# One decoder layer on one core: MLP up projection in pairs of output tiles by Strassen's scheme

## The chip, the cores and the metric

The kernel runs on one core of a Trainium2 chip. The metric is device time in microseconds (us). The times of the kernel before, from three runs, are 928.68, 927.98 and 928.27 us, median 928.27. The engines are named PE (matrix products), DVE (vector), ACT (scalar functions), POOL (GpSimd) and SP (issues DMAs). PSUM is the memory that PE adds into, in banks of 512 fp32 columns; SBUF holds everything else on chip.

## The reference, cut to what matters

```python
xn = rms_norm(h, g_mix[i])
z = xn @ w_in[i]
...
h = h + (gate_a * ya + gate_b * yb) @ w_o[i]
hn = rms_norm(h, g_mlp[i])
h = h + jnp.square(jax.nn.relu(hn @ w_up[i])) @ w_down[i]
gp = jax.nn.sigmoid(rms_norm(h, g_ple[i]) @ w_ple_gate[i])
h = h + gp * (p[i] @ w_ple_proj[i])
```

There is one layer, 1024 channels, an MLP of 4096, and 576 tokens (512 of a prompt and 8 x 8 samples). `w_up` is 1024 x 4096 and `w_down` 4096 x 1024. Everything is fp32.

## The kernel before

Channels lie on partitions and tokens on columns, in two halves of 288. `product` (L104) makes one output tile of 128 channels x 576 tokens: for each of 8 k tiles it does three matmuls, since every fp32 operand is split into two parts, hi + lo, and hi x hi, hi x lo and lo x hi are added up (`mm`, L99). Each matmul is done for both halves, into two banks of one PSUM tile. So a tile takes 8 x 3 x 2 = 48 matmuls of 128 x 288. Four PSUM tiles of two banks take turns.

The weights of one output tile are one unit, 128 x 1024, read from memory by SP (`load_unit`, L81). `split` makes hi on ACT (L70) and lo on DVE (L71). Four raw units and three split ones fit. `Stream.next` splits two units ahead of use and loads one more ahead. So the order in which units stand in `order` and the place of `next()` in the program set when ACT and DVE split, between the other work on their queues. Each engine runs its queue in the order of the program.

Stages, with their stretch in the profiled execution: the first products, k by k as the loads land (0 to 31 us), the convolution branch (31 to 160), its gate and projection (160 to 262), the pooling branch (262 to 390), w_o (390 to 434), then the MLP in four blocks of 8 up and 8 down tiles (434 to 846; the first up stage is 434 to 488, the second 539 to 590, the third 641 to 692), and the embedding gate and last norm. In the first stage, `stat.tokens()` (L235 to L244) and `stat.spread()` (L251) make 1/rms of each token between the products: sums on PE, then a chain of small operations on ACT and DVE, then PE spreads them.

In w_o the residual is added by DVE (L404) and the operand of the MLP is made by `split_act` with the gain (L73, L74). In an up tile ACT takes the relu from PSUM (L421), DVE squares it (L423), and it is split (L70, L71). A down tile is added up on DVE (L437).

## Time and profile before

| | before |
|---|---|
| median of 3 runs | 928.27 us |
| profiled execution, span | 926.5 us |
| PE busy | 913.4 us, 99% of the span |
| DVE busy | 431.6 us, 47% |
| ACT busy | 289.8 us, 31% |
| POOL busy | 98.3 us, 11% |
| bytes by SP's queue | 79.98 MB, 26.4% of the DMA engines' time |

The time of the profiled execution itself is given only as its span, from the first to the last instruction. PE's clock is at its full level in all of the 40 slices but the last. Busy times count what an engine works on; an engine with a low share can still hold up another, if the order on its queue is unlucky. The chain of waits is followed from the last instruction back, so a long piece of it on one engine means that this engine had no gap there.

### The profile page before, as it was taken

The numbers are of one execution on the slowest core, as the hardware profiler recorded it, in microseconds if no ns is written. First come the engines' busy times: TensorE is split into PE (matmuls) and PEld (weight loads), VectorE is DVE, ScalarE is ACT, GpSimd is POOL, SyncE is SP. The second block draws the span as 40 slices with busy tenths as digits, with TensorE's granted clock in tenths as the row PEclk, the third lists the DMA queues.
The fourth block names the chain that finished last, engine by engine and source line by source line (L and its number), as shares of the span: only waits on it lengthen the run. The fifth ranks groups of instructions, "written<-read, shape, count | busy, mean of one in ns | idle before, by whom it ended". The sixth has DMA issues, their size and how long they took to land.

```text
span 926.5 us, 15543 instructions
## 1 busy us (share of the span) xinstructions
PE 913.4 (99%) x6842; PEld 911.5 (98%) x6842; DVE 431.6 (47%) x570; ACT 289.8 (31%) x384; POOL 98.3 (11%) x118
## 2 busy tenths in 40 slices
PE   8999999999999999999999999999999999999995
PEld 7999999999999999999999999999999999999995
DVE  7645445333246687743342133332443334567555
ACT  6422212322113222333433233211331133335532
POOL 5110001000011221023000000000000000021253
PEclk9999999999999999999999999999999999999997
DMA  6422222322322222322222222222222222222102
GB/s 227 155 92 76 84 92 69 94 88 73 92 61 88 68 92 96 112 79 91 69 90 71 91 79 82 91 70 91 87 73 92 74 86 92 94 92 84 54 22 82
DMA packets 26290, 80.98 MB, mean 87 GB/s; under 512 B 3312, under 2 KB 7024, under 8 KB 26224
## 3 DMA queue, kind: packets, MB, share of 16 engines
q1 hardware_dynamic: 26080, 79.98, 26.4%
q8 instruction: 53, 0.87, 0.4%
q14 instruction: 13, 0.11, 0.0%
q10 hardware_dynamic: 144, 0.03, 0.0%
HBM read 77.01 MB, written 2.99 MB: 86 GB/s over the span
## 4 chain that ended last, share of the span: by engine, by line
PE 97%; DVE 1%; issue 1%; DMA 1%; SPq 0%; DVEq 0%; ACT 0%; ACTq 0%
PE ps L99 89%; PE psg L99 6%; PE psf L99 1%; PE psn L251 1%; DVE lo L71 1%; DMA xall<-x 1%; PE psn L235 1%; DVE xall L464 0%; SPq L169 0%; DVE lo L74 0%; SPq L163 0%; DVEq L564 0%; DVE gp L491 0%; DVE xall L493 0%; DVE sq L218 0%
## 5 line engine op out<-in xcount | busy, mean ns | idle before, releaser
L99 PE MATMUL ps<-lo,hi 128*128 128x288 f32 x2064 | 442.2, 296 | 0.0
L99 PE MATMUL ps<-hi 128*128 128x288 f32 x2064 | 442.1, 296 | 0.0
L99 PE MATMUL ps<-hi,lo 128*128 128x288 f32 x2064 | 441.8, 296 | 0.0
L99 PEld LDWEIGHTS ps<-hi,lo 128*128 128x128 f32 x2064 | 332.7, 189 | 0.0
L99 PEld LDWEIGHTS ps<-lo,hi 128*128 128x128 f32 x2064 | 332.7, 189 | 0.0
L99 PEld LDWEIGHTS ps<-hi 128*128 128x128 f32 x2064 | 332.6, 189 | 0.0
L70 ACT CAST hi<-raw 128x1024 fp32r<-128x1024 f32 (+1 forms) x144 | 144.8, 1008 | 468.3 <-PE ps L99 400.9
L71 DVE TENSOR_TENSOR lo<-raw,hi 128x1024 fp32r<-128x1024 f32 (+1 forms) x144 | 169.3, 1179 | 157.0 <-ACT hi L70 150.4
L437 DVE TENSOR_TENSOR acc<-ps,acc 128x576 f32<-128x576 f32 x24 | 18.2, 758 | 74.3 <-PE ps L99 74.3
L225 POOL TENSOR_TENSOR ss<-sq 128x576 f32<-128x576 f32 (+2 forms) x5 | 7.2, 1434 | 416.4 <-ACT sq L220 416.4
L225 POOL TENSOR_TENSOR ss<-ss,sq 128x576 f32<-128x576 f32 (+2 forms) x29 | 38.5, 1327 | 70.3 <-ACT sq L220 56.8
L99 PE MATMUL psg<-hi 128*128 128x320 f32 (+1 forms) x128 | 38.1, 298 | 0.0
L99 PE MATMUL psg<-lo,hi 128*128 128x320 f32 (+1 forms) x128 | 37.9, 296 | 0.0
L99 PE MATMUL psg<-hi,lo 128*128 128x320 f32 (+1 forms) x128 | 37.9, 296 | 0.0
L71 DVE TENSOR_TENSOR lo<-a,hi 128x576 fp32r<-128x576 f32 x32 | 24.3, 759 | 23.6 <-ACT hi L70 23.6
L70 ACT CAST hi<-a 128x576 fp32r<-128x576 f32 x32 | 21.6, 675 | 43.6 <-DVE a L423 43.6
L220 ACT ACTIVATE sq<-xall 128x576 f32<-128x576 f32 (+2 forms) x39 | 22.7, 585 | 19.5 <-DVE xall L493 19.5
L74 DVE SCALAR_TENSOR_TENSOR lo<-xall,vec,hi 128x576 fp32r<-128x576 f32 x23 | 21.7, 946 | 7.9 <-ACT hi L73 7.9
L99 PEld LDWEIGHTS psg<-hi 128*128 128x128 f32 x128 | 24.3, 190 | 0.0
L99 PEld LDWEIGHTS psg<-lo,hi 128*128 128x128 f32 x128 | 24.3, 190 | 0.0
L99 PEld LDWEIGHTS psg<-hi,lo 128*128 128x128 f32 x128 | 24.3, 190 | 0.0
L423 DVE TENSOR_TENSOR a<-a 128x576 f32<-128x576 f32 x32 | 24.1, 752 | 0.0
(98 smaller groups left out, 444.3 us busy)
## 6 DMA issues: line engine op xcount, KB each, us to landing
raw<-w_in SPq DMA_DIRECT2D x45, 512.0 KB, 3.4
raw<-w_up SPq DMA_DIRECT2D x32, 512.0 KB, 3.4
raw<-w_down SPq DMA_DIRECT2D x32, 512.0 KB, 3.5
raw<-w_oc SPq DMA_DIRECT2D x8, 512.0 KB, 3.4
raw<-w_o SPq DMA_DIRECT2D x8, 512.0 KB, 3.5
raw<-w_pg SPq DMA_DIRECT2D x8, 512.0 KB, 3.5
xall<-x SPq DMA_DIRECT2D x7, 288.0 KB, 5.2
fraw<-w_first SPq DMA_DIRECT2D x8, 192.0 KB, 5.1
```

Source lines behind the costliest of these rows:

```text
L70: nc.scalar.copy(hi, src)
L71: nc.vector.tensor_tensor(out=lo, in0=src, in1=as32(hi), op=ALU.subtract)
L74: nc.vector.scalar_tensor_tensor(out=lo, in0=src, scalar=scale, in1=as32(hi), op0=ALU.mult, op1=ALU.subtract)
L99: nc.tensor.matmul(o, wt, cols(at), start=start and i == 0, stop=stop and i == 2)
L220: nc.scalar.activation(sq, t, AF.Square)
L225: nc.gpsimd.tensor_tensor(out=s, in0=self.parts[0], in1=sq, op=ALU.add)
L235: nc.tensor.matmul(sums[:, i:i + 1], a[:, h, c:c + m], ones32[:, 0:1], start=k == 0, stop=k == len(self.parts) - 1)
L251: nc.tensor.matmul(self.ps[:, h, c:c + m], self.y[:, i:i + 1].broadcast_to([m, P]), idt[:m, :m], start=True, stop=True)
L423: nc.vector.tensor_tensor(out=a2, in0=a, in1=a, op=ALU.mult)
L437: nc.vector.tensor_tensor(out=accs[j], in0=halves(ps), in1=accs[j], op=ALU.add)
```

## The change

The 8 up tiles of a block form four pairs, q and q + 4. Of a pair, the weights are two units of 128 x 1024, cut in halves of the k tiles: a and b of the first, c and d of the second. The operand is cut in halves of k and halves of the tokens. Strassen's scheme (in Winograd's form) makes the 2 x 2 block product with seven products of quarters. A quarter is 4 k tiles x 3 passes = 12 matmuls of 128 x 288 into one bank (L481), a pair so 84. The order of the products is b11, t2, t3, t1, b21 (added to the first product in its bank), the first product b11 of the next pair, t4 and b22 (added to their banks). The banks of a pair are those of two PSUM tiles, ab and cd; t2 and b11 are in ab, t3, t1, t4 and b22 in cd.

The operand's sums (t1 to t4) are made once, in w_o, by `Operand.add` (ACT: the gain; DVE: L505, L507, L508; splits L80, L502), for which w_o's outputs come in the order 0, 4, 1, 5, ... The weights' sums are made for each pair: s1 = c + d and s0 = c + a by a load on SP and a second DMA on POOL's queue that adds (L140), s2 = s1 + a on DVE (L160) and s3 = -s2 - b on DVE (L162). Seven forms are split a pair. Between the products ACT copies the first product (L519), and DVE takes the sums of products from PSUM: L532 (reads t2's bank), L534 (t3's), L536 (t1's), and after the last product L557. Then follow the relus and the square on ACT (L586 to L591).

All weights come in parts of 512 columns, eight raw and seven split ones, loaded five parts ahead. In the first pair of block 0 and in the first two down tiles of each block the last k tile's products are put later. The sums of squares are added on POOL in place, and the working buffers are pools that are closed between parts of the kernel. Two places of the diff are left out here: the same renaming of `stream.next()` to `stream.take(2)` in every other stage, and the pools' names.

```diff
+KH = D // 2
+NQ = NJ // 2
+NF = 7
...
-    wraw = ctx.enter_context(tc.tile_pool(name="wraw", bufs=4))
-    wsp = ctx.enter_context(tc.tile_pool(name="wsp", bufs=3))
-    tmp = ctx.enter_context(tc.tile_pool(name="tmp", bufs=8))
+    wraw = ctx.enter_context(tc.tile_pool(name="wraw", bufs=8))
+    wsp = ctx.enter_context(tc.tile_pool(name="wsp", bufs=NF))
...
+    def raw_tile(ap):
+        raw = wraw.tile([P, KH], F32, tag="raw", name="raw")
+        nc.sync.dma_start(raw, ap)
+        return raw
...
+        def summed(self, x, y):
+            raw = raw_tile(x)
+            nc.gpsimd.dma_start(raw, y, accum_op=ALU.add)
+            return raw
...
+    class Form:
+        def __init__(self, pair, name):
+            self.pair, self.name = pair, name
+
+        def load(self):
+            p, name = self.pair, self.name
+            if name in ("a", "b", "d"):
+                setattr(p, "r" + name, raw_tile(getattr(p, name)))
+            elif name == "s2":
+                p.rs1 = p.summed(p.c, p.d)
+            elif name == "s0":
+                p.rs0 = p.summed(p.c, p.a)
+
+        def split(self):
+            p, name = self.pair, self.name
+            if name == "s2":
+                p.rs2 = tmp.tile([P, KH], F32, tag="s", name="s2", bufs=2)
+                nc.vector.tensor_tensor(out=p.rs2, in0=p.rs1, in1=p.ra, op=ALU.add)
+            elif name == "s3":
+                nc.vector.scalar_tensor_tensor(
+                    out=p.rs2, in0=p.rs2, scalar=-1.0, in1=p.rb, op0=ALU.mult, op1=ALU.subtract)
+            return split(p.rs2 if name == "s3" else getattr(p, "r" + name), [P, KH], wsp, "w")
...
+        def take(self, n=1, live=0):
+
+            first = self.used - live
+            for i in range(n):
+                splits = min(self.used + n + NF - 1, first + NF)
+                self.fill(splits + self.loads, splits)
+            out = self.parts[self.used:self.used + n]
+            for i in range(self.used, self.used + n):
+                self.parts[i] = self.items[i] = None
+            self.used += n
+            return out
...
+    halved = [i + h * NQ for i in range(NQ) for h in range(2)]
+    for j in halved:
+        order += unit(w_o[j])
     for b in range(NFB):
-        order += [w_up[b * NJ + j] for j in range(NJ)]
-        order += [w_down[b * NJ + j] for j in range(NJ)]
-    order += [w_pp[i] for i in range(2)]
-    order += [w_pg[j] for j in range(NJ)]
-    stream = Stream(order, resident=range(len(order) - NJ, len(order) - 3))
-
-    # ---- loads: the input and the first weights by k tiles, so that products start early ----
+        pairs = [Pair(w_up[b * NJ + q], w_up[b * NJ + NQ + q]) for q in range(NQ)]
+        order += [Form(pairs[0], "a")]
+        for q in range(NQ):
+            order += [Form(pairs[q], n) for n in ("s2", "s0", "s1", "b")]
+            if q + 1 < NQ:
+                order += [Form(pairs[q + 1], "a")]
+            order += [Form(pairs[q], n) for n in ("d", "s3")]
...
+        raw = wraw.tile([P, KH], F32, tag="raw", name="fraw")
+        fraw.append(raw[:, :3 * P])
...
-    stream.fill(3, 0)
+    stream.fill(6, 0)
...
-                s = tmp.tile(self.shape, F32, tag="t", name="ss")
-                nc.gpsimd.tensor_tensor(out=s, in0=self.parts[0], in1=sq, op=ALU.add)
-                self.parts[0] = s
+                nc.gpsimd.tensor_tensor(out=self.parts[0], in0=self.parts[0], in1=sq, op=ALU.add)
...
+    def quarter(o, w, bs, ks, start, stop):
+        for k in ks:
+            wh, wl = (t[:, k * P:(k + 1) * P] for t in w)
+            hi, lo = bs[k]
+            for i, (wt, at) in enumerate(((wh, hi), (wh, lo), (wl, hi))):
+                nc.tensor.matmul(o, wt, at, start=start and k == 0 and i == 0,
+                                 stop=stop and k == NQ - 1 and i == 2, skip_group_check=True)
+    class Operand:
+        def __init__(self):
+            self.f = {n: [None] * NQ for n in ("b11", "b22", "b21", "t1", "t3", "t2", "t4")}
+            self.shared = None
+        def two(self, k, src, names):
+            parts = split(src, [P, NH, HT], acts2 if k == 0 else acts, "act")
+            for i, n in enumerate(names):
+                self.f[n][k] = tuple(t[:, i] for t in parts)
+        def add(self, k, g):
+            if k % 2 == 0:
+                self.shared = tuple(acts.tile([P, NH, HT], F32R, tag="act", name=n) for n in ("hi", "lo"))
+            self.two(k, g[:, 1:3], ("b11", "b22"))
+            hi, lo = (t[:, k % 2] for t in self.shared)
+            nc.scalar.copy(hi, g[:, 3])
+            nc.vector.tensor_tensor(out=lo, in0=g[:, 3], in1=as32(hi), op=ALU.subtract)
+            self.f["b21"][k] = hi, lo
+            t = tmp.tile([P, 4, HT], F32, tag="g", name="gt", bufs=2)
+            nc.vector.tensor_tensor(
+                out=t[:, 0:2], in0=g[:, 0:1].broadcast_to([P, 2, HT]), in1=g[:, 1:3], op=ALU.subtract)
+            nc.vector.tensor_tensor(out=t[:, 2], in0=g[:, 2], in1=t[:, 0], op=ALU.subtract)
+            nc.vector.tensor_tensor(out=t[:, 3], in0=g[:, 3], in1=t[:, 2], op=ALU.subtract)
+            self.two(k, t[:, 0:2], ("t1", "t3"))
+            self.two(k, t[:, 2:4], ("t2", "t4"))
+    def pairs_of(n, op, corner, finish, late=False, between=None):
+        def begin(w):
+            ab = psum.tile([P, NH, 512], F32, tag="ps", name="ab")
+            quarter(ab[:, 0, :HT], w, op.f["b11"], range(NQ), True, True)
+            g = tmp.tile([P, 4, HT], F32, tag="g", name="g", bufs=2)
+            nc.scalar.copy(g[:, 1], ab[:, 0, :HT])
+            return ab, g
+        ab, g = begin(stream.take()[0])
+        for i in range(n):
+            cd = psum.tile([P, NH, 512], F32, tag="ps", name="cd")
+            pa, pb, pc, pd = ab[:, 0, :HT], ab[:, 1, :HT], cd[:, 0, :HT], cd[:, 1, :HT]
+            u2 = tmp.tile([P, 1, HT], F32, tag="u", name="u", bufs=1)
+            u = u2[:, 0]
+            todo = ((pb, "t2"), (pd, "t3"), (pc, "t1"))
+            def middle(x):
+                if x == 0:
+                    nc.vector.tensor_tensor(out=u, in0=pb, in1=g[:, 1], op=ALU.subtract)
+                elif x == 1:
+                    nc.vector.tensor_tensor(out=g[:, 2], in0=pd, in1=u, op=ALU.add)
+                else:
+                    nc.vector.tensor_tensor(out=g[:, 2], in0=pc, in1=g[:, 2], op=ALU.add)
+            if late and i == 0:
+                ws = []
+                for x, (o, name) in enumerate(todo):
+                    ws += stream.take(live=x)
+                    quarter(o, ws[x], op.f[name], range(NQ - 1), True, True)
+                quarter(pa, stream.take(live=3)[0], op.f["b21"], range(NQ), False, True)
+                for x, (o, name) in enumerate(todo):
+                    quarter(o, ws[x], op.f[name], range(NQ - 1, NQ), False, True)
+                    middle(x)
+            else:
+                for x, (o, name) in enumerate(todo):
+                    quarter(o, stream.take()[0], op.f[name], range(NQ), True, True)
+                    middle(x)
+                quarter(pa, stream.take()[0], op.f["b21"], range(NQ), False, True)
+            corner(i, g, pa)
+            if i + 1 < n:
+                after = begin(stream.take()[0])
+            quarter(pd, stream.take()[0], op.f["t4"], range(NQ), False, True)
+            quarter(pc, stream.take()[0], op.f["b22"], range(NQ), False, True)
+            nc.vector.tensor_tensor(
+                out=g[:, 0::3], in0=halves(cd), in1=u2.broadcast_to([P, 2, HT]), op=ALU.add)
+            finish(i, g)
+            if i + 1 < n:
+                ab, g = after
+            if between:
+                between(i)
...
+    for x, j in enumerate(halved):
+        ps = product(stream.take(2), merged)
         nc.vector.tensor_tensor(out=xs[j], in0=halves(ps), in1=xs[j], op=ALU.add)
+        if x % 2 == 0:
+            g = tmp.tile([P, 4, HT], F32, tag="g", name="gx", bufs=2)
+        nc.scalar.mul(g[:, 2 * (x % 2):2 * (x % 2) + 2], xs[j], v(G_MLP, j))
+        if x % 2:
+            hg.add(x // 2, g)
...
+        def corner(q, g, c11):
+            nc.scalar.activation(g[:, 1], c11, AF.Relu)
+        def finish(q, g):
+            nc.scalar.activation(g[:, 0], g[:, 0], AF.Relu, scale=-1.0)
+            nc.scalar.activation(g[:, 2:4], g[:, 2:4], AF.Relu)
+            nc.scalar.activation(g, g, AF.Square)
+            sq[q] = split_act(g[:, 0:2])
+            sq[q + NQ] = split_act(g[:, 2:4])
+        def between(q):
+            if b == 0 and q == 0:
                 stat.tokens()
+            if b == 0 and q == 1:
+                stat.r2s = stat.copies(stat.spread(), "r", "rs")[1]
+        pairs_of(NQ, hg, corner, finish, b == 0, between)
...
+            if j == 0:
+                two = [stream.take(2), stream.take(2, live=2)]
+                two = [(w, psum.tile([P, NH, 512], F32, tag="ps", name="ps")) for w in two]
+                for ks in (halved[:-2], halved[-2:]):
+                    for w, ps in two:
+                        steps(ps, w, sq, ks, first=halved[0], last=halved[-1])
+            if j < 2:
+                ps = two[j][1]
+            else:
+                ps = product(stream.take(2), sq)
```

DVE near the start, before: the splits of the first weights (fraw), of the first streamed units (raw), and the chain that makes 1/rms (ms, ry, rz).

```order
L71 TENSOR_TENSOR lo<-fraw,hi 128x384 x2
L71 TENSOR_TENSOR lo<-raw,hi 128x1024
L240 TENSOR_SCALAR ms<-psn 96x6
L241 RECIPROCAL ry<-rt 96x6
L242 TENSOR_TENSOR rz<-ry 96x6
L243 SCALAR_TENSOR_TENSOR rz<-rz,ms 96x6
L244 SCALAR_TENSOR_TENSOR ry<-rz,ry 96x6
L71 TENSOR_TENSOR lo<-raw,hi 128x1024
L286 TENSOR_TENSOR c<-psf,rs 128x576
```

And now the same place:

```order
L80 TENSOR_TENSOR lo<-fraw,hi 128x384
L80 TENSOR_TENSOR lo<-raw,hi 128x512 x5
L312 TENSOR_SCALAR ms<-psn 96x6
L313 RECIPROCAL ry<-rt 96x6
L314 TENSOR_TENSOR rz<-ry 96x6
L315 SCALAR_TENSOR_TENSOR rz<-rz,ms 96x6
L316 SCALAR_TENSOR_TENSOR ry<-rz,ry 96x6
L80 TENSOR_TENSOR lo<-raw,hi 128x512
L358 TENSOR_TENSOR c<-psf,rs 128x576
```

One split of 1024 columns stood ahead of the chain, and now five of 512 do.

DVE in an up stage, before: two output tiles of the second block, weight split, square (a) and its split.

```order
L71 TENSOR_TENSOR lo<-raw,hi 128x1024
L423 TENSOR_TENSOR a_6823<-a 128x576
L71 TENSOR_TENSOR lo<-a_6823,hi 128x576
L71 TENSOR_TENSOR lo<-raw,hi 128x1024
L423 TENSOR_TENSOR a_6886<-a 128x576
L71 TENSOR_TENSOR lo<-a_6886,hi 128x576
```

Now one pair of the second block. s is the weights' sum, u and g hold sums of products, ab and cd are PSUM.

```order
L80 TENSOR_TENSOR lo<-s_6068,hi 128x512
L532 TENSOR_TENSOR u<-ab,g 128x288
L160 TENSOR_TENSOR s_6362<-raw 128x512
L80 TENSOR_TENSOR lo<-s_6216,hi 128x512
L534 TENSOR_TENSOR g<-cd,u 128x288
L162 SCALAR_TENSOR_TENSOR s_6216<-s_6216,raw 128x512
L80 TENSOR_TENSOR lo<-raw,hi 128x512
L80 TENSOR_TENSOR lo<-g,hi 128x576
L536 TENSOR_TENSOR g<-cd,g 128x288
L80 TENSOR_TENSOR lo<-g,hi 128x576
L80 TENSOR_TENSOR lo<-raw,hi 128x512 x4
L557 TENSOR_TENSOR g<-cd,u 128x2x288
```

The reads of PSUM stand between weight splits and sums of the pair after next: L160, which reads a sum made by the DMA on POOL, now stands ahead of L534.

PE in an up stage, before, with what each waits for, at the end of one tile and the begin of the next.

```order
L99 MATMUL ps_6282<-hi_5936,hi_6166 128x288 x2
L99 MATMUL ps_6282<-lo_5937,hi_6166 128x288 x2
L99 MATMUL ps_6282<-hi_5936,lo_6167 128x288 x2
L99 MATMUL ps_6338<-hi_5495,hi_6222 128x288 [waits Activation_49]
L99 MATMUL ps_6338<-hi_5495,hi_6222 128x288
L99 MATMUL ps_6338<-lo_5496,hi_6222 128x288 x2
L99 MATMUL ps_6338<-hi_5495,lo_6223 128x288 [waits DVE_49]
L99 MATMUL ps_6338<-hi_5495,lo_6223 128x288
```

Now in the second pair of the second block, at the end of t3 (into cd), where t1 (into cd) follows.

```order
L481 MATMUL cd_6192<-hi_4885,hi_6087 128x288
L481 MATMUL cd_6192<-lo_4886,hi_6087 128x288
L481 MATMUL cd_6192<-hi_4885,lo_6088 128x288
L481 MATMUL ab_6131<-hi_4416,hi_6127 128x288 [waits DVE_49]
L481 MATMUL ab_6131<-lo_4417,hi_6127 128x288
L481 MATMUL ab_6131<-hi_4416,lo_6128 128x288
L481 MATMUL ab_6131<-hi_4416,hi_6127 128x288
L481 MATMUL ab_6131<-lo_4417,hi_6127 128x288
L481 MATMUL cd_6192<-hi_4428,hi_6107 128x288 [waits DVE_49]
L481 MATMUL cd_6192<-lo_4429,hi_6107 128x288
```

A new tile waited for its weights' hi and lo; now t1 waits for a DVE operation that reads t3's bank, and five matmuls of b21 are put ahead of it, the first with a wait for DVE as well.

## Rows read from the trace of the kernel before

**Rows 1.** The page: busy time of each engine, share of the span and instructions; and the chain that ended last, its share by engine.

```profile
PE 913.4 (99%) x6842; PEld 911.5 (98%) x6842; DVE 431.6 (47%) x570; ACT 289.8 (31%) x384; POOL 98.3 (11%) x118
...
PE 97%; DVE 1%; issue 1%; DMA 1%; SPq 0%; DVEq 0%; ACT 0%; ACTq 0%
```

**Rows 2.** The chain that ended last, in order of time: start, duration (both us), engine, tile, line and count. ps is an output tile, psn the statistics, psf the first products, psg the last gate.

```profile
24.86 2.88 PE psf L99 x21
27.75 1.31 PE psn L251 x12
31.08 409.60 PE ps L99 x3072
...
449.41 403.22 PE ps L99 x3024
861.37 33.22 PE psg L99 x234
...
899.27 14.81 PE psg L99 x123
```

**Rows 3.** Windows of the second and the third up stage: the stretch, its length, then busy us and instructions of PE, PE's weight load, DVE, ACT and POOL; the granted clock of PE, the DMA share and GB/s.

```profile
539.00:590.00 51.00, 51.00 (x385) 51.00 (x384) 19.80 (x22) 17.30 (x23) 0.00 (x0) 1.00 0.26 84
...
641.00:692.00 51.00, 51.00 (x385) 51.00 (x384) 20.56 (x23) 16.97 (x22) 0.00 (x0) 1.00 0.26 83
```

**Rows 4.** Groups of instructions by line and shape: line, engine, operation, tiles and shapes, count; then busy us, mean ns of one; then idle time ahead. The splits of weights, and an operation of DVE on 512 columns with both inputs in SBUF.

```profile
L71 DVE TENSOR_TENSOR lo<-raw,hi 128x1024 fp32r<-128x1024 f32 x130 | 159.2, 1225 | 154.9 <-ACT hi L70 148.3
L70 ACT CAST hi<-raw 128x1024 fp32r<-128x1024 f32 x130 | 136.5, 1050 | 461.1 <-PE ps L99 393.7 <-issue 62.2 <-DVE lo L71 3.1
L71 DVE TENSOR_TENSOR lo<-raw,hi 128x512 fp32r<-128x512 f32 x14 | 10.1, 750 | 2.1 <-ACT hi L70 2.1
L70 ACT CAST hi<-raw 128x512 fp32r<-128x512 f32 x14 | 8.4, 619 | 7.2 <-PE ps L99 7.2
L361 DVE SCALAR_TENSOR_TENSOR pl<-q,e 128x512 f32<-128x512 f32 x8 | 5.5, 693 | 0.3
```

**Rows 5.** The same view for operations on 256 to 576 columns; the last two rows are from the timeline of DVE (start, duration), an operation and the next one.

```profile
L484 DVE TENSOR_TENSOR z<-psg,r 128x320 f32<-128x320 f32 x8 | 3.9, 491 | 8.6 <-PE psg L99 8.6
L484 DVE TENSOR_TENSOR z<-psg,r 128x256 f32<-128x256 f32 x8 | 3.4, 419 | 3.2 <-PE psg L99 3.2
L404 DVE TENSOR_TENSOR xall<-ps,xall 128x576 f32<-128x576 f32 x8 | 6.1, 758 | 26.4 <-PE ps L99 26.4
L71 DVE TENSOR_TENSOR lo<-a,hi 128x576 fp32r<-128x576 f32 x32 | 24.3, 759 | 23.6 <-ACT hi L70 23.6
L421 ACT ACTIVATE a<-ps 128x576 f32<-128x576 f32 x32 | 20.6, 644 | 0.0
L70 ACT CAST hi<-a 128x576 fp32r<-128x576 f32 x32 | 21.6, 675 | 43.6 <-DVE a L423 43.6
L220 ACT ACTIVATE sq<-xall 128x320 f32<-128x320 f32 x8 | 3.8, 471 | 9.9 <-DVE xall L493 9.9
L73 ACT ACTIVATE hi<-xall,vec 128x576 fp32r<-128x576 f32 x23 | 17.8, 773 | 19.4 <-DVE xall L440 19.3
...
902.80 1.01 DVE L464 TENSOR_TENSOR xall<-xall,r 128x640 f32<-128x640 f32 x1
903.73 0.41 DVE L493 TENSOR_TENSOR xall<-gp,xall 128x256 f32<-128x256 f32 x1
```

**Rows 6.** DMA issues: tile and source, queue, count, KB each and median us from issue to landing.

```profile
raw<-w_up SPq DMA_DIRECT2D x32, 512.0 KB, 3.4
...
xall<-x SPq DMA_DIRECT2D x7, 288.0 KB, 5.2
...
raw<-w_pool SPq DMA_DIRECT2D x4, 256.0 KB, 2.7
pin<-pt SPq DMA_DIRECT2D x2, 288.0 KB, 4.2
```

**Rows 7.** The timeline at the end of the start: start and duration in us, engine, line, operation; in brackets the idle time ahead and what ended it.

```profile
23.61 0.55 DVE L71 TENSOR_TENSOR lo<-fraw,hi 128x384 fp32r<-128x384 f32 x1
...
24.78 1.23 DVE L71 TENSOR_TENSOR lo<-raw,hi 128x1024 fp32r<-128x1024 f32 x1 [0.62 <-ACT hi L70]
...
26.35 0.16 DVE L240 TENSOR_SCALAR ms<-psn 96x6 f32<-96x6 f32 x1 [0.35 <-ACT rt L239]
...
27.04 0.16 DVE L244 SCALAR_TENSOR_TENSOR ry<-rz,ry 96x6 f32<-96x6 f32 x1
...
27.58 1.47 PE L251 MATMUL psn<-idt,ry 96*128 96x96 f32 x12
```

**Rows 8.** The timeline around 12.7 us: five additions of POOL one after the other, and a split on DVE beside them.

```profile
12.69 8.65 POOL L225 TENSOR_TENSOR ss<-ss,sq 128x576 f32<-128x576 f32 x5 [1.00 <-ACT sq L220]
...
12.77 1.79 DVE L71 TENSOR_TENSOR lo<-fraw,hi 128x384 fp32r<-128x384 f32 x1
```

More of the change, by code (lines that the diff above doesn't have):

```diff
@@ L102, in both, with steps @@
         return [(ps[:, h, :HT], lambda t, h=h: t[:, h, :]) for h in range(NH)]
+    def steps(ps, unit, operands, ks, base=0, m=P, step=P, first=None, last=None):
+        for k in ks:
+            mm(both(ps), unit, base + k * step, m, operands[k], k == first, k == last)
     def product(unit, operands, base=0, m=P, step=P):
@@ L107, in product, with __init__ @@
         n = len(operands)
[L108 to L111 removed]
+        steps(ps, unit, operands, range(n), base, m, step, 0, n - 1)
+        return ps
+    def raw_tile(ap):
+        raw = wraw.tile([P, KH], F32, tag="raw", name="raw")
+        nc.sync.dma_start(raw, ap)
+        return raw
+    class Part:
+        def __init__(self, ap, resident=False):
+            self.ap, self.resident = ap, resident
+        def load(self):
+            self.raw = raw_tile(self.ap)
+        def split(self):
+            pool, tag = (acts, "act") if self.resident else (wsp, "w")
+            w = split(self.raw, [P, KH], pool, tag)
+            self.raw = None
+            return w
@@ L127, in next @@
-        def next(self):
-            self.fill(self.used + 1 + self.ahead + 1, self.used + 1 + self.ahead)
-            self.used += 1
-            w = self.parts[self.used - 1]
-            self.parts[self.used - 1] = self.raws[self.used - 1] = None
-            return w
+            n = len(self.items)
+            while self.nload < min(loads, n):
+                self.items[self.nload].load()
+                self.nload += 1
+            while len(self.parts) < min(splits, n):
+                self.parts.append(self.items[len(self.parts)].split())
@@ new lines, in take, with unit @@
+        def take(self, n=1, live=0):
[8 more added lines that the diff above has]
+            return out
+    def unit(ap):
+        return [Part(ap[:, i:i + KH]) for i in range(0, ap.shape[1], KH)]
@@ L152, in tile_hybrid_step @@
+    for i in range(2):
+        order += unit(w_pp[i])
+    for j in range(NJ):
+        order += [Part(w_pg[j][:, i:i + KH], resident=j < NJ - 3) for i in range(0, D, KH)]
+    stream = Stream(order)
     vec = const.tile([P, NV, NJ], F32, tag="vec", name="vec")
@@ L306, in tile_hybrid_step @@
                 op0=ALU.mult, op1=ALU.add)
-        ps_b = ps0[2] if j == 0 else product(stream.next(), xg)
+        ps_b = ps0[2] if j == 0 else product(stream.take(2), xg)
         bt = tmp.tile([P, NH, HT], F32, tag="t", name="bt")
@@ L323, in tile_hybrid_step @@
     for j in range(NJ):
-        ps = product(stream.next(), xg)
+        ps = product(stream.take(2), xg)
         z = tmp.tile([P, NH, HT], F32, tag="t", name="z")
@@ L330, in tile_hybrid_step @@
     for j in range(NJ):
-        ps = product(stream.next(), ya_in)
+        ps = product(stream.take(2), ya_in)
         nc.vector.tensor_tensor(out=mix[j], in0=halves(ps), in1=mix[j], op=ALU.mult)
@@ L339, in tile_hybrid_step @@
             j = 2 * g + i
-            ps = product(stream.next(), xg)
+            ps = product(stream.take(2), xg)
             e = tmp.tile([P, PEXT], F32, tag="ext", bufs=4, name="e")
@@ L379, in tile_hybrid_step @@
         for i in range(2):
-            ps = product(stream.next(), xg)
+            ps = product(stream.take(2), xg)
             z = tmp.tile([P, NH, HT], F32, tag="t", name="zb")
@@ L385, in tile_hybrid_step @@
             gates.append(gb)
-        wp = stream.next()
+        wp = stream.take()
         for i in range(2):
@@ L446, in tile_hybrid_step @@
     for i in range(2):
-        w = stream.next()
+        w = stream.take(2)
         for m in range(NJ // 2):
```

109 lines of the change are left out of this document (48 added, 61 removed).

## The prediction

> **What bounds the kernel now.** I read the page's busy shares first: TensorE (PE) is busy 913.4 of 926.5 us and VectorE (DVE) less than half of that [rows 1]. The reader is to see there that only work taken from PE, or a gap put into it, can move the time. The chain of work that ended last says the same: 97% of it is PE [rows 1]. Its pieces give the price of the unit of work. In 409.60 us stand 3072 matmuls of 288 columns, in 403.22 us 3024, so one takes 133.3 ns and from 31 to 853 us nothing waits [rows 2]. Then I read the stages by windows, because the shares of the page average over stages. An up block runs from 539 to 590 us: PE fills it, DVE works 19.80 and ScalarE (ACT) 17.30 of 51.00 us [rows 3]. This room is what the change spends.
>
> The sum is made against the span of the profiled execution, 926.5 us; no other time of that execution is given. The median of the three runs is 928.27, 1.8 us above, and I add this 1.8 at the end unchanged.
>
> **What goes.** A pair of output tiles takes 96 matmuls now and 84 after it: 7 quarters of 4 k tiles and 3 passes. There are 4 blocks of 4 pairs: 16 x 12 = 192 matmuls fewer, x 133.3 ns = 25.6 us. The floor is so 926.5 - 25.6 = 900.9, or 902.7 us on the scale of the median.
>
> The matmul keeps its shape, but a quarter sums twelve in a row into one bank, where before two banks took turns. The last stage does this already: 123 matmuls of 256 columns in 14.81 us, 120.4 ns each [rows 2]. 256/288 of 133.3 is 118.5, so a single bank costs nothing I can see (2 ns at most, 2.7 us over 1344 quarter matmuls). I take nothing.
>
> **What DVE and ACT get.** Per pair, DVE now has seven lo splits of 512 columns, the sum for s2, the one for s3, three operations on 288 columns of PSUM, the last addition on 2 x 288, and two lo splits of activations. A 512-column operation with both inputs in SBUF took 0.693 (L361); the fourteen lo splits of that size had a mean of 0.750 [rows 4]. I take 0.69. For 288 columns from PSUM I take 0.455, midway between 256 (0.419) and 320 (0.491); for 576 columns 0.76 [rows 5]. Sum: 9 x 0.69 + 3 x 0.455 + 3 x 0.76 = 9.9 us, against 84 x 0.1333 = 11.2 us of PE. Before, a pair took two tiles' share, 19.80 / 51.00 x 12.8 = 5.0 of 12.8 us. ACT gets seven casts (0.619), a copy and two relus of 288 columns (0.47 by the 320-column row), one relu of 576 (0.644), a square of 1152 (two of 0.644) and two casts (0.675): some 9 us [rows 4, 5]. Neither engine is the bound, but DVE goes from 39% to 88%, so an operation that PE waits for may have to stand behind another.
>
> **Waits inside a pair.** Three new ones can reach PE. t2 needs ACT's copy L519 of the first product; b21 needs L532, which reads t2's bank; t1 needs L534, which reads t3's bank, because the two banks are one tile. Behind t1's wait stands all of PE's queue. The order has five b21 matmuls (0.67 us) between t3 and t1, and L534 takes 0.455 plus two handovers. Free DVE: about no wait. DVE in the middle of a split: up to 0.69 more. I take 0.15 a pair as the usual case. In the first pair of blocks 1 to 3 the copy stands behind a 576-column cast on ACT and L534 behind two splits: 0.75. That is 0.75 + 3 x 0.15 = 1.2 a block, 3.6 in all. From below, all hidden, it is 0; from above, no operation overlapping another, 2.5 a block or 7.5.
>
> **Seam and first block.** After the last output of w_o, DVE and ACT must make all operand forms of the last k tile: L570, the gain on ACT, gt, L507, a lo split, L502, L508, another lo split. By rows that is 0.76 + 0.77 + 0.76 + 0.455 + 0.76 + 0.455 + 0.455 + 0.76 = 5.2 us, plus some 0.4 of handovers [rows 5]. The order puts 38 matmuls, 5.1 us, ahead of the one that needs the end of it. So 0.5 is exposed, and I add 0.5 for the three other pairs of block 0: +1.0, between 0.2 and 2.2 (one operation late on each engine, more than once).
>
> **The start.** Now the last lo of the first weights ends at 24.16 us, one 1024-column split follows, and the statistics chain on DVE runs from 26.35 to 27.20; PE's spread follows at 27.58 behind the products [rows 7]. In the new order five 512-column splits stand ahead of the chain. DVE's operations follow each other 0.08 us before the recorded end of the one ahead [rows 5], so five take 5 x 0.61 = 3.05: the chain goes from 27.2 to 28.05. PE has come to its spread, which now stands right behind k = 6, at about 24.72 + 18 x 0.133 = 27.1. It stands 0.9 us. By 0.75 a split it would be 1.6; with the splits waiting for nobody but fitting in earlier gaps, 0.
>
> **The accumulating DMAs.** s1 and s0 are made in memory: a plain load on SP, then a second DMA on POOL's queue that adds. 32 of them, none with a row in this trace: every data DMA here goes by SP or ACT [rows 6]. What matters is its time from issue to landing, X. In the second pair of blocks 1 to 3 DVE's L160, which reads the finished s1 for the last pair, stands ahead of L534. Counting back by the durations above, the raw buffer comes free 3.4 us before that pair starts, the load lands 2.7 later, POOL issues at -0.55, and DVE arrives at L160 at +2.2. So X may be 2.75; each us above it goes on DVE, then, through L534, on PE, three times. The other L160s have 5.1 us and more. The nearest rows are a plain 256 KB load, 2.7, and 288 KB, 4.2 and 5.2 when many transfers ran; the accumulation reads two times 256 KB, and a 512 KB load takes 3.4 [rows 6]. I take X = 3.4: 3 x 0.65 = 2.0 us. At 2.7 it is 0, at 5.2 it is 7.4 (and past that all L160s join).
>
> The Trainium skill has a price for this path: "DMA: Bandwidth & Descriptors", section on the anatomy of a DMA by the gpsimd path, gives about 2.0 us plus the bytes over 436,000 per us, which I make 2.6 us for 256 KB, an estimate. No row here shows it; by it this wait is gone and the sum is 2.0 us less.
>
> **Sum.** 926.5 - 25.6 + 3.6 + 1.0 + 0.9 + 2.0 = 908.4, plus 1.8: **910.2 us**. The terms' lower ends give 902.9, their upper ends together 926.5 - 25.6 + 7.5 + 2.2 + 1.6 + 7.4 + 1.8 = 921.4; they will not all be at one end, so this case's own range is 905.5 to 919.
>
> **Rivals.** (B) All waits are hidden, only the start shows: 902.7 + 0.9 = 903.6. For it: DVE is 12% free and PE's order has fillers. Against: several of these fillers are as long as the operations they hide, with nothing over.
>
> (C) The wait chain binds every pair: t1 behind L534 and t4 behind L536, each an operation of 0.455 and 0.2 of handovers with no filler, because the filler is used up by the split ahead on DVE. 2 x 0.655 x 16 = 21.0: 902.7 + 0.9 + 21.0 = 924.6, from 919 if half of the waits are partly covered. For it: 88% load on one queue served in order. Against: behind t1 stand seven b21 matmuls and the next pair's twelve, 2.5 us, before t4 needs L536.
>
> (D) The other side: the accumulating DMA is slow, because POOL must prepare it while DVE works nearly without a pause. The trace shows what the two do to each other: while POOL added, DVE's 384-column split took 1.79 us, alone 0.55 [rows 7, 8]. With X = 9: 3 x 6.25 + 3 x (9 - 5.1) + (9 - 5.7) for the first block = 33.8 us in place of 2.0, so 942.0. From X of about 7 on the gain is gone. Against: POOL runs nothing else in the up stages, 0.00 us in 539 to 590 [rows 3].
> The Trainium skill states such a lock in "SBUF — State Buffer", the box on DVE blocking a DMA of GpSimd's queue; the longer DVE splits beside POOL's additions agree with a contention, though not for a DMA.
>
> (E) Matmuls into one bank are slower in the quarters than in the last stage; 13 to 19 ns more each would eat the gain (1344 x 19 = 25.5 us). The last stage speaks against it.
>
> **How the numbers follow.** The summed case 0.56, B 0.13, C 0.14, D 0.13, E 0.04. A measurement of this kernel can tell 0.2%, 1.9 us, from no change. The first two and most of C (0.11) are faster, and with a little of D and E that is 0.82; the end of C, D about X = 7 and E give 0.05 for no change; the rest of D and half of E are 0.13 slower. The range goes from B to the end of C, 903.5 to 927, and leaves out most of D and E and a little of B.
>
> **What would show it.** Right: PE's matmuls of the up stages fall to 1344 at 133 ns; an up block takes 46 to 48 us instead of 51; idle time of PE before t1 is put down to L534, and L160 waits for a DMA from POOL by under 1 us, in second pairs only. Wrong: DVE idle on a POOL DMA in every pair (D); idle PE before both t1 and t4 in every pair (C); quarter matmuls well over 133 ns apart without a wait (E); a start that ends where it did.

## The result and the profile after

Median of four runs 919.02 us (917.03 to 923.70) against 928.44; ratio 0.9908, 95% interval 0.9881 to 0.9935. The kernel is 9.4 us faster, where 18.1 were forecast. The time lies in the range of the forecast, the gain is about half of the forecast one (8.5 us by the ratio). Of one run below, that with three edits together, two of six executions took 4943.83 and 1234.35 us, for no reason that a trace shows, and its numbers are of the other four.

The profiled execution is the longest of the four: span 921.9, 923.7 us by its own time. The page's busy shares and the chain's shares by engine, beside [rows 1]:

```profile
PE 898.6 (97%) x6650; PEld 893.6 (97%) x6650; DVE 521.3 (57%) x832; ACT 370.1 (40%) x626; POOL 113.4 (12%) x150
...
PE 92%; DMA 3%; ACT 2%; DVE 2%; issue 1%; POOL 0%; SPq 0%; DVEq 0%; POOLq 0%
```

PE has 192 matmuls fewer, and still bounds the kernel, but 3% of the chain is now a DMA, where there was none but the first load. The chain by its long pieces shows where the time went, as [rows 2] did (start, duration, engine, tile, line, count; ps L95 is a run of down tiles, but x3024 that of all stages up to w_o; ab and cd L481 are up pairs):

```profile
31.92 403.21 PE ps L95 x3024
...
484.90 50.92 PE ps L95 x382
...
545.63 3.51 DMA raw<-w_up
549.21 0.49 issue
549.70 4.26 DMA raw<-w_up
554.04 0.10 DVE s L160
554.25 0.41 issue
554.65 0.68 DVE lo L80
555.34 0.38 DVE g L534
555.76 2.23 PE cd L481 x12
557.99 3.67 PE ab L481 x19
...
586.10 50.92 PE ps L95 x382
...
657.04 3.25 PE cd L481 x12
660.29 3.72 PE ab L481 x19
...
688.42 50.92 PE ps L95 x382
...
790.75 57.32 PE ps L95 x430
```

The reader is to see two things. First, from one long run of down tiles to the next lie 720 matmuls, 96.0 us at 133.3 ns; it is 101.2, 102.3 and 102.3 us in blocks 1 to 3, so 5.2, 6.3 and 6.3 us are lost. Second, each block has one broken place, in its second pair: a load that waited for a buffer, the adding DMA on POOL, L160, a split, L534, and only then PE. The view of what PE waited for gives the sum of it (us, times, longest):

```profile
PE cd L481 <- DVE g L534: 8.6, 3, 2.9
...
PE cd L481 <- DVE lo L80: 1.4, 1, 1.4
```

And after the wait PE is slow. 12 matmuls take 1.6 us; behind the waits they took 2.23, 3.25 and 3.25, and the next 19 (2.53) 3.67, 3.72 and 3.77. Together 7.5 us. The windows around the second wait (columns as in [rows 3]) show why: PE does nothing up to 657.0, where its granted clock already falls (0.64 on the average). Then the clock is 0.50, the lower level of 1.2 GHz, and it comes back only within the stretch behind 660.3:

```profile
655.60:657.00 1.40, 0.00 (x0) 0.00 (x0) 1.40 (x4) 0.00 (x0) 0.00 (x0) 0.64 0.24 42
657.00:660.30 3.30, 3.26 (x13) 3.27 (x14) 1.85 (x3) 0.22 (x1) 0.00 (x0) 0.50 0.27 73
660.30:664.00 3.70, 3.70 (x21) 3.70 (x21) 2.42 (x4) 1.42 (x4) 0.00 (x0) 0.66 0.20 66
```

The sum for this execution: 926.5 - 25.6 + 0.84 (the start: 31.08 in [rows 2], now 31.92) + 2.45 (the seam: 49.77 us from 435.13, the end of w_o, to 484.90, less 338 matmuls, 45.07, and the statistics, 2.25) + 17.8 (blocks 1 to 3) = 922.0. The span is 921.9.

### The profile page after: what moved, and what is told of

The parts are those of the page before. It is cut to its first block, busy times and chain, and to the rows that moved or that the text cites. A ratio compares the mean times of both kernels' runs of the same rounds, so it can differ in the third digit from the quotient of the medians.

```text
span 921.9 us, 16512 instructions
## 1 busy us (share of the span) xinstructions
PE 898.6 (97%) x6650; PEld 893.6 (97%) x6650; DVE 521.3 (57%) x832; ACT 370.1 (40%) x626; POOL 113.4 (12%) x150
## 4 chain that ended last, share of the span: by engine, by line
PE 92%; DMA 3%; ACT 2%; DVE 2%; issue 1%; POOL 0%; SPq 0%; DVEq 0%; POOLq 0%
PE ps L95 67%; PE cd L481 10%; PE ab L481 7%; PE psg L95 6%; DMA raw<-w_up 2%; PE psf L95 1%; PE psn L323 1%; DVE lo L80 1%; ACT hi L79 1%; ACT hi L82 0%; PE psn L307 0%; POOL sq L298 0%; ACT sq L294 0%; DMA xall<-x 0%; DVE xall L653 0%
## 5 line engine op out<-in xcount | busy, mean ns | idle before, releaser
L79 ACT CAST hi<-raw 128x512 fp32r<-128x512 f32 x290 | 177.8, 619 | 404.7 <-PE ps L95 325.9
L95 PE MATMUL ps<-hi,lo 128*128 128x288 f32 x1552 | 332.7, 296 | 0.0
L95 PE MATMUL ps<-lo,hi 128*128 128x288 f32 x1552 | 332.6, 296 | 0.0
L95 PE MATMUL ps<-hi 128*128 128x288 f32 x1552 | 332.5, 296 | 0.0
L80 DVE TENSOR_TENSOR lo<-raw,hi 128x512 fp32r<-128x512 f32 x290 | 203.7, 710 | 151.9 <-ACT hi L79 150.4
L95 PEld LDWEIGHTS ps<-hi,lo 128*128 128x128 f32 x1552 | 250.2, 189 | 0.0
L95 PEld LDWEIGHTS ps<-hi 128*128 128x128 f32 x1552 | 250.1, 189 | 0.0
L95 PEld LDWEIGHTS ps<-lo,hi 128*128 128x128 f32 x1552 | 250.1, 189 | 0.0
L481 PE MATMUL cd<-hi 128*128 128x288 f32 x256 | 78.2, 306 | 8.8 <-DVE g L534 8.6
L481 PE MATMUL cd<-lo,hi 128*128 128x288 f32 x256 | 77.0, 301 | 1.4 <-DVE lo L80 1.4
L481 PE MATMUL cd<-hi,lo 128*128 128x288 f32 x256 | 77.0, 301 | 0.0
L140 POOL DMA_DIRECT2D raw<-w_up x32 | 27.9, 879 | 330.8 <-DVE lo L80 154.0
L481 PEld LDWEIGHTS cd<-hi 128*128 128x128 f32 x256 | 49.1, 192 | 10.6 <-DVE g L534 9.4
L481 PE MATMUL ab<-hi 128*128 128x288 f32 x192 | 59.1, 308 | 0.0
L481 PE MATMUL ab<-hi,lo 128*128 128x288 f32 x192 | 58.3, 305 | 0.0
L481 PE MATMUL ab<-lo,hi 128*128 128x288 f32 x192 | 58.1, 302 | 0.0
L481 PEld LDWEIGHTS cd<-lo,hi 128*128 128x128 f32 x256 | 49.4, 193 | 1.6 <-DVE lo L80 1.6
L481 PEld LDWEIGHTS cd<-hi,lo 128*128 128x128 f32 x256 | 49.4, 193 | 0.0
L481 PEld LDWEIGHTS ab<-hi 128*128 128x128 f32 x192 | 37.8, 197 | 1.5 <-ACT g L519 0.7
L95 PE MATMUL psg<-hi 128*128 128x320 f32 (+1 forms) x128 | 38.2, 298 | 0.0
L481 PEld LDWEIGHTS ab<-hi,lo 128*128 128x128 f32 x192 | 37.9, 198 | 0.0
```

The lines of the kernel that those rows point to most:

```text
L79: nc.scalar.copy(hi, src)
L80: nc.vector.tensor_tensor(out=lo, in0=src, in1=as32(hi), op=ALU.subtract)
L95: nc.tensor.matmul(o, wt, cols(at), start=start and i == 0, stop=stop and i == 2)
L140: nc.gpsimd.dma_start(raw, y, accum_op=ALU.add)
L481: nc.tensor.matmul(o, wt, at, start=start and k == 0 and i == 0, stop=stop and k == NQ - 1 and i == 2, skip_group_check=True)
```

## The experiments

Each is an edit of the changed kernel and is compared with the kernel before on its own chip (926.5 to 927.8 us). Short diffs; the line numbers in the profiles move by a few where lines were added.

**Without the sum.**

```diff
-            nc.gpsimd.dma_start(raw, y, accum_op=ALU.add)
```

> The second, adding DMA on POOL's queue is left out, so s1 and s0 hold only c (that part of the computation is missing). Theory (late sum): in the changed kernel the second pair of blocks 1 to 3 stands 2.9 us each on the sum, 8.6 in all, and PE's lower clock behind it costs 0.63 + 1.65 + 1.65 for t1 and 1.14 + 1.19 + 1.24 for the 19 matmuls after it, 7.5 us. Without the DMA both go: span 921.9 - 16.1 = 905.8, time about 907.5. Rival (full DVE queue): L534 is late because DVE has 88% of its time taken; then waits show up at other splits and the time stays at 914 or more.

906.93 us against 926.47; ratio 0.9794 (0.9779 to 0.9808). L534 isn't waited for any more, and blocks 1 to 3 take 96.7 us each; the first of them:

```profile
486.27 50.92 PE ps L95 x382
...
582.95 50.92 PE ps L95 x382
```

So all else in a block, DVE's full queue included, costs 0.7 us, and the rest of the 17.8 us hung on the adding DMA.

**A copy in place of the sum.**

```diff
-            nc.gpsimd.dma_start(raw, y, accum_op=ALU.add)
+            nc.gpsimd.dma_start(raw, y)
```

> The second DMA on POOL's queue only copies and doesn't add (the sums are replaced by their second term). It tells what makes X long. Path theory: the way over POOL costs the time; X stays at 4.2 to 4.8 us, the three waits at 2.6 to 3.0 us and the time at 917 to 923. Adding theory: reading the buffer and adding costs it; X falls to 2.7 to 3.4, the waits to 1.5 or less, and the time to 911 or below.

913.94 us, ratio 0.9869 (0.9854 to 0.9883). The DMA rows of the changed kernel (columns as in [rows 6]):

```profile
raw<-w_up SPq DMA_DIRECT2D x80, 256.0 KB, 2.9
...
raw<-w_up POOLq DMA_DIRECT2D x32, 256.0 KB, 4.6
```

and of this one, in which PE waited for L534 three times, 5.0 us in all:

```profile
raw<-w_up SPq DMA_DIRECT2D x80, 256.0 KB, 2.7
...
raw<-w_up POOLq DMA_DIRECT2D x32, 256.0 KB, 3.4
```

Neither theory alone: the way over POOL costs 0.7 us more than a load by SP, the adding 1.2 more. Behind two of the three waits (2.2 and 1.8 us) the clock fell to 0.50, behind the third (1.1) it did not.

**Something to do for PE while it waits.**

```diff
                 for x, (o, name) in enumerate(todo):
-                    quarter(o, stream.take()[0], op.f[name], range(NQ), True, True)
+                    w = stream.take()[0]
+                    if i == 1 and x == 2 and not late:
+                        for _ in range(24):
+                            nc.tensor.matmul(pb, w[0][:, :P], op.f[name][0][0], start=True, stop=True, skip_group_check=True)
+                    quarter(o, w, op.f[name], range(NQ), True, True)
                     middle(x)
```

> 24 matmuls whose result nobody reads (3.2 us) are put into PE's queue ahead of t1 in the second pair of blocks 1 to 3, where PE stands. Theory (stall and clock add up): the wait for L534 stays on DVE but PE pauses only briefly, its clock stays at its upper level, and the 7.5 us go: time 911 to 914, all granted clock 1.00 between 550 and 790. Rival (no clock cost, only the wait): the time stays as it was, 917 to 923, or is up to 1 us longer, since the five matmuls that stood there move behind.

919.40 us, ratio 0.9918 (0.9902 to 0.9935): not the 911 to 914 of the theory. In the trace the clock did what was said. Windows over the same place in blocks 1 to 3 (the granted clock is the third number from the end):

```profile
550.00:560.00 10.00, 10.00 (x77) 10.00 (x77) 6.68 (x12) 5.90 (x10) 1.72 (x2) 1.00 0.54 119
650.00:660.00 10.00, 8.52 (x65) 8.28 (x64) 5.14 (x9) 5.02 (x9) 1.75 (x2) 1.00 0.54 113
750.00:760.00 10.00, 10.00 (x76) 9.79 (x75) 5.83 (x10) 5.85 (x11) 1.73 (x2) 1.00 0.64 152
```

The three blocks take 99.8, 101.5 and 100.0 us, 4.6 less in all than in the changed kernel, though 9.6 us of matmuls were put in. They lose 13.3 us to 3 x 96.0, and the 9.6, a wait of 1.5 that is left and 3 x 0.7 make 13.2: nothing is left for the clock. But the start and the seam took 0.6 and 1.9 us longer here (at the seam the clock was at 0.50 behind a wait of 1.7 us), and the theory had compared with the profiled execution, which is the longest of its four. The mean clocks of the four executions of the changed kernel are 0.984, 0.992, 0.992 and 0.991 with 923.70, 917.03, 917.79 and 920.25 us; 0.008 of 920 is 7.4 us, and 6.7 lie between the first and the second. So the lower clock costs more in some executions than in others: about 7 us more in the profiled one than in the one of 917.03, whose whole gap to the kernel without the sum is 7.7 us by the ratios (0.9877 and 0.9794), no more than the waits alone. There is no trace of that execution, so this division is argued from the clocks.

**The same DMA, but another queue waits for it.**

```diff
-                nc.vector.tensor_tensor(out=p.rs2, in0=p.rs1, in1=p.ra, op=ALU.add)
+                nc.gpsimd.tensor_tensor(out=p.rs2, in0=p.rs1, in1=p.ra, op=ALU.add)
```

> The changed kernel as it is, but s2 = s1 + a (L160) is made by POOL in place of DVE. The DMA and its X stay; only the queue that waits for it is another. Theory (what costs is L534 standing behind the waiting L160): L534 comes in time, PE's waits for it go (8.6 us before), and with them the lower clock: 907 to 911. Rival (whoever makes s2, its split comes too late for t2 of the next pair, or POOL's additions slow DVE's splits as in rows 8): PE waits for lo splits or ACT, 914 or more.

908.89 us, ratio 0.9798 (0.9785 to 0.9812). X is 4.6 as before (median of its DMA row), DMA and buffers are the same, and the loss is gone: 96.7 us a block in the chain.

```profile
485.04 50.92 PE ps L95 x382
...
581.72 50.92 PE ps L95 x382
```

What POOL waited for in L160 (us, times, longest):

```profile
POOL s L160 <- DMA raw<-w_up: 26.4, 8, 3.8
```

POOL now waits 26.4 us for the sums, and PE for none of it. POOL takes 1.45 us for the addition that DVE made in 0.69, and DVE's splits of g become longer (0.88 us, 0.75 before), but PE waits for neither in blocks 1 to 3. This is the cleanest separation of the study: not the DMA's time cost the gain, but what was queued behind the instruction that waited for it.

**Earlier by one buffer, by a deeper queue, by two buffers.** Three ways to get the sum sooner and leave L160 on DVE:

```diff
-            if name in ("a", "b", "d"):
+            if name == "a":
+                p.rs1 = p.summed(p.c, p.d)
+            if name in ("a", "b", "d"):
                 setattr(p, "r" + name, raw_tile(getattr(p, name)))
-            elif name == "s2":
-                p.rs1 = p.summed(p.c, p.d)
```

> The load of c and the adding DMA for s1 are issued one raw buffer earlier (with the load of a, not after it). At 5 raw buffers a pair of 11.2 us this is 2.2 us. Late sum theory: the waits of 2.9 become 0.7 or nothing, the clock stays up, and the time is 921.9 - 6.6 - 7.5 + 1.8 = 909.6, or 907.5 if nothing is left. Rival (POOL's queue or DVE limits): the DMA is issued earlier but lands no earlier, or s0's takes its place: 915 or more.

915.52 us, ratio 0.9883 (0.9869 to 0.9898). Blocks 1 to 3 take 98.8, 98.0 and 97.8 us, so about a third of the loss was left. The time is the rival's, the way is another: the order now puts L160 ahead of L532, and PE waited for L532 three times, 2.6 us in all, and once 2.3 us for ACT. In w_o, block 0's sum was late as well (a DMA of 5.45 us in the chain).

```diff
-NF = 7
+NF = 6
-    wraw = ctx.enter_context(tc.tile_pool(name="wraw", bufs=8))
+    wraw = ctx.enter_context(tc.tile_pool(name="wraw", bufs=10))
-        def __init__(self, items, loads=5):
+        def __init__(self, items, loads=7):
```

> The changed kernel with six split parts ahead in place of seven, ten raw ones in place of eight, and loads seven parts ahead of the splits in place of five: the same memory, but each sum is loaded two raw buffers, some 4.4 us, earlier. Late sum theory: the waits of L160 for the DMA (2.9 us each) go, and with them the lower clock; what stays is what stayed without the DMA: 907 to 910 against 926.5 before. Rival (six splits ahead are too few): PE waits for lo splits: 912 or more.

913.86 us, ratio 0.9865 (0.9828 to 0.9901): a miss. Counted from the end of the down tiles, the loads start 0.6 to 0.8 us earlier, not 4.4, since each still waits for the split that frees its buffer, and the sum then takes longer:

```profile
641.62 0.70 DVE lo L80
642.34 2.68 DMA raw<-w_up
645.09 0.48 issue
645.59 6.32 DMA raw<-w_up
651.98 0.17 DVE s L160
```

Why X is up to 6.3 us here is open. Loads by SP issued beside the sums of blocks 2 and 3 took 5.4 to 5.9 us, where their median is 2.7 to 2.9, so the transfers may slow one another; no run tests it. PE still waited for L534 in three places, and this time its clock stayed at 1.00 behind all of them:

```profile
PE cd L481 <- DVE g L534: 5.0, 3, 2.3
```

The third way issues s1 of the next pair with b of this one, in blocks 1 to 3, and has the change of the seam (next) in it:

```diff
+            if name == "b" and p.follow:
+                p.follow.rs1 = p.follow.summed(p.follow.c, p.follow.d)
...
-            elif name == "s2":
+            elif name == "s2" and not p.led:
                 p.rs1 = p.summed(p.c, p.d)
```

> Seven splits and eight raw buffers as in the changed kernel, but in blocks 1 to 3 the load and the adding DMA of s1 for the next pair are issued two raw buffers earlier, and the seam as in the run before it. Late sum theory: waits for L160 gone, 906 to 909. Rival: holding the sum's buffer longer delays the other loads by as much, and PE waits for lo splits instead: 912 or more.

908.35 us (908.07 to 909.18), ratio 0.9789 (0.9774 to 0.9804). Blocks take 96.7 us each as without the sum, and no wait of t1, t4 or b21 is listed. In its up stages PE stands no more. DVE is busy for 33.59 us of a stretch of 47.00 that holds a few down tiles too, 71%, where the forecast gave it 88% of a pair.

```profile
537.00:584.00 47.00, 47.00 (x350) 46.25 (x349) 33.59 (x55) 29.72 (x53) 2.59 (x3) 1.00 0.48 134
```

**The seam.** An edit of the kernel with ten raw buffers:

```diff
-        stat.add(xs[j])
+        stat.add(xs[j], own=x == NJ - 1)
...
-            if last or not self.parts:
+            if last or own or not self.parts:
```

> The same, and the last of the eight squares at the end of w_o isn't added by POOL but goes to PE as a second summand (six more matmuls of one column). Theory (contention at the seam): the last 288-column split took 2.0 us in the changed kernel beside POOL's addition, against 0.45 alone, and PE stood 1.4 us behind it; without that addition it takes 0.45 to 0.7 and the run is 1.0 to 2.0 us shorter than the one before it here. Rival (the seam is the chain of operations itself, 5.2 us by the sum): within 0.4 us.

915.05 us, ratio 0.9859 (0.9842 to 0.9875) against 0.9865: nothing by the times, whose runs spread over 5 to 10 us with their clocks (0.984 to 0.996). The traces tell it. In the changed kernel, DVE and POOL at the seam:

```profile
438.60 2.00 DVE L502 TENSOR_TENSOR lo<-gx,hi 128x288 fp32r<-128x288 f32 x1
...
438.52 1.76 POOL L298 TENSOR_TENSOR sq<-sq 128x576 f32<-128x576 f32 x1
```

and here, without POOL's addition:

```profile
438.25 0.45 DVE L502 TENSOR_TENSOR lo<-gx,hi 128x288 fp32r<-128x288 f32 x1
```

L502 began 0.08 us behind POOL's addition and ended 0.3 behind it; it took 2.00, and 0.45 without it. This is [rows 8] again, now ahead of PE. The Trainium skill, "SBUF — State Buffer", section on the two separate sides, has a DVE operation with two inputs in SBUF and a GpSimd operation that reads SBUF shut each other out for the whole instruction; these rows agree.

But little of it is won. PE waits nowhere at the seam any more, where it stood 0.94 us in the run before, yet 24 matmuls of one column make the statistics, not 12, and take 1.96 us in place of 0.94. From the end of w_o to the first long run of down tiles it is 48.9 us against 49.4. And the three other runs with this edit (the one before, the one on the start and the last one) took 50.5, 51.1 and 50.5 us for it: in each the clock fell to 0.50 right behind these matmuls of one column. Windows of this run and of the one before:

```profile
447.00:453.00 6.00, 6.00 (x47) 6.00 (x46) 4.49 (x13) 3.01 (x7) 1.75 (x2) 1.00 0.74 203
```

```profile
447.00:453.00 6.00, 6.00 (x38) 6.00 (x38) 2.60 (x9) 2.48 (x5) 0.00 (x0) 0.72 0.67 218
```

PE is busy in all of both stretches; its granted clock is 1.00 in one and 0.72, on the average, in the other.

**The parts alone, and the start.** The weights in parts with the up projection as before (the diff is cut to the up projection; the order of the weights, w_o as it was, and six working buffers in place of three go with it):

```diff
-        pairs_of(NQ, hg, corner, finish, b == 0, between)
+        for j in range(NJ):
+            ps = product(stream.take(2), hg)
...
+            a = tmp.tile([P, NH, HT], F32, tag="t", name="a")
+            nc.scalar.activation(a, halves(ps), AF.Relu)
+            a2 = tmp.tile([P, NH, HT], F32, tag="t", name="a2")
+            nc.vector.tensor_tensor(out=a2, in0=a, in1=a, op=ALU.mult)
+            sq.append(split_act(a2))
```

> One part of the change alone: weights in 512-column parts, eight raw and seven split, and the sums of squares in place, but the up projection as in the kernel before (48 matmuls a tile) and w_o in its old order. Theory: it costs only the start, where five splits stand ahead of the statistics (0.9 us by the sum, 0.84 in the trace of the changed kernel): 0.5 to 1.2 us slower than before, all of it in the first 32 us. Rival: halving the operations costs DVE and ACT so much that PE waits in other stages too: 3 us or more.

929.59 us against 927.79, ratio 1.0009 (0.9979 to 1.0040). The interval is wide because one execution of before and two of this were some 9 us shorter than all others, for no reason that the records show. By the medians it is 1.8 us slower. In the trace the stretch of 3072 matmuls begins at 31.94, 0.86 later than in [rows 2], and nothing is lost behind it; the other 0.9 us is not found. Then the start itself, on the kernel with s1 two buffers earlier:

```diff
-    stream.fill(6, 0)
+    stream.fill(2, 0)
```

> The kernel of the run before (s1 two raw buffers earlier, the last square to PE) with only two in place of six parts of the streamed weights loaded ahead of the constants at the start, so that two splits of 512 columns, not five, stand on DVE ahead of the chain for 1/rms. Theory (the start is the splits ahead of the chain): 3 x 0.61 = 1.8 us less ahead of the chain; the 0.84 us that the start was longer goes, 0.5 to 1.2 us shorter than 0.979 of before, so 0.9775 to 0.9785. Rival (loads come too late): PE waits for the first streamed weights behind 32 us, and nothing is won or it is slower.

909.01 us, ratio 0.9797 (0.9781 to 0.9812): no gain by the times. In the trace the chain for 1/rms ends at 26.1 in place of 27.8 and the first products at 30.56. The pieces of the chain, of the changed kernel and of this one:

```profile
22.98 1.18 PE psn L307 x12
24.16 4.03 PE psf L95 x18
28.18 1.31 PE psn L323 x12
29.49 2.43 PE psf L95 x18
```

```profile
23.15 1.18 PE psn L313 x12
24.33 2.50 PE psf L95 x18
26.83 1.31 PE psn L329 x12
28.14 2.42 PE psf L95 x18
```

In the changed kernel's execution PE's granted clock was 0.58 on the average from 24.16 to 28.18, behind a wait of 1.5 us for POOL's additions, so 18 matmuls took 4.03 us in place of 2.4 and PE came to its spread at 28.2, later than the chain, which ended at 27.8. With the clock up, as in the run on the seam, PE came early and stood 0.57 us for the chain, until 27.57, and the first products ended at 31.57, 0.49 later than before. So of the 0.84 some 0.35 came from the clock in that execution, an estimate from these two runs.

**All three together** (s2 by POOL, the seam, the start):

> The three together that showed a gain in the traces: s2 by POOL, the last square of w_o to PE, and two parts loaded ahead of the constants at the start. Theory (the three are in different stretches and add up): against the run with s2 by POOL alone (span 906.1) the seam gives 1.5 and the start 0.8 to 1.4, so a span of 903.2 to 904 and 0.974 to 0.976 of before. Rival (the stretches hide one another, or the start's gain is given back by later loads): 0.978 to 0.980 as in the runs before.

906.02 to 909.56 us, median 908.2; ratio 0.9782 (0.9767 to 0.9796). The interval takes in the ratio of s1 two buffers earlier (0.9789) and overlaps that of s2 by POOL alone (0.9785 to 0.9812), so it isn't shown that the three add up. Its trace (span 907.8) has the low clock in both places, at the start (18 matmuls in 3.97 us) and behind the 24 matmuls, and so neither gain. With the run of 908.35 it is the fastest form found: some 20 us under the kernel before, 11 to 12 under the changed one by the ratios.

## Where the prediction was right and where it failed

**What failed, in short.** One term failed by its size: the accumulating DMAs, put at 2.0 us. They cost 16.1 us in the profiled execution, 8.6 of waits and 7.5 of PE's lower clock behind them, and 10.6 over all executions (ratio 0.9908, and 0.9794 without the adding DMA). The clock's part was put at nothing, without a reason.

**What goes: right.** 192 matmuls at 133.3 ns; with the sums' wait gone, blocks 1 to 3 take 96.7 us of 96.0 possible. One bank costs nothing (24 matmuls of cd in 3.19 us, 132.9 ns each): rival E is out.

**DVE and ACT: the durations were right.** L532, L534 and L536 took 0.457, 0.452 and 0.455 us (0.455 taken), L160 0.691 (0.69), L557 0.758 (0.76); L162 was longer, 0.805 (0.69). Waits inside a pair cost 0.7 a block, not 1.2; rival C is out.

**The accumulating DMA: right place, wrong size.** It was named for the second pair of blocks 1 to 3, with L160 ahead of L534, and that is where it reached PE. Three pieces of the term failed.

- X was taken at 3.4, the value of a load of 512 KB. In the three places it was 4.3 to 4.8 (median of all 4.6), of which the adding is 1.2.
- The time that X may take was taken as 2.75 us and was 1.45. Counted from the pair's first t2 matmul (548.91 in block 1), the buffer came free at -3.3 (-3.4 forecast) and DVE came to L160 at +2.2 (as forecast). But the load took 3.5 us, not 2.7, and POOL began 0.5 behind its landing, so at +0.8, not at -0.55. With X = 4.6 and 1.45 the sum's own formula gives 3 x 3.15 = 9.5 for the 8.6 measured.
- The term had no price for PE's clock behind a wait: 7.5 us.

The signs moved with it. An up stage took 50.0 to 51.1 us, not 46 to 48, and 45.5 without the sum. And DVE waited at 11 of the 16 L160s, not in second pairs only; PE felt the three in the second pairs (us, times, longest):

```profile
DVE s L160 <- DMA raw<-w_up: 31.9, 11, 5.4
```

The price from the Trainium skill, "DMA: Bandwidth & Descriptors", section on the anatomy of a DMA by the gpsimd path, gives an estimate of 2.6 us for 256 KB by POOL's path; here a copy took 3.4 and a sum 4.6, so the row's bounds, 2.7 to 5.2, held it and the page's price did not.

Rival D, the slow DMA, had the right direction but not the mechanism: X does not go with DVE's load. The sum issued at 401.77 landed in 4.0 us with DVE busy all the time, the one issued at 603.14 in 5.1 us with DVE idle throughout, and POOL was busy with the two for 0.88 and 0.86 us.

**The seam: 1.0 forecast, 2.45 measured.** The working had every operation at its length alone. POOL's addition of the last square, in the same stretch, made one of them 1.5 us longer, and PE stood 1.4 us for the splits; [rows 8] showed that, and it was used only for rival D.

**The start: 0.9 forecast, 0.84 measured.** The number is luck in part: some 0.35 of it is the clock in the profiled execution, and the chain alone made it 0.49 later in the run where the clock stayed up.

Without the DMA's term the forecast's sum is 908.2, and the runs that do without that wait have ratios of 0.9782 to 0.9798, 908.0 to 909.5 us at the 928.27 of before. That agreement too is luck in part: the seam cost 1.45 us more than forecast, and the waits inside the pairs 1.5 less (2.1 in place of 3.6).

## What to carry to other kernels

An instruction that waits costs what stands behind it on its queue. When a transfer of unknown length feeds an engine that PE also needs, give the wait to an engine that nobody waits for, or issue the transfer two buffers sooner; shortening the transfer won less here (3.6 us by the ratios, where these won 10 to 11). And a wait of 2 to 3 us of PE is priced with the slow stretch that can follow it, which about doubled it in one execution here and was absent in others.
